# Splits of the last operands on GpSimd at a later place, source order of three engines at the first tiles, and another order of the last scalings

## The chip, the cores and the metric

One NeuronCore of a Trainium2 chip runs the whole program. Its engines work side by side, each from a queue of its own: TensorE (PE in the profile; its weight loads are PEld), VectorE (DVE), ScalarE (ACT), GpSimd (POOL), and SyncE (SP), which here only issues DMA transfers. The metric is the device time of one execution in microseconds, the median over runs.

## The reference

One layer of a hybrid decoder on 1024 tokens of width 1024, in float32:

```
u = rmsnorm(x, g0);  z = u @ w_in              # 1024 x 6048
o_attn = dilated attention of 3 head groups    # windows 128, 512, 2048; strides 1, 4, 16
o_rwkv = RWKV-7 time mixing of z               # 8 heads of 64, delta-rule state
merged = sigmoid(gate_a) * (o_attn @ w_attn_up) + sigmoid(gate_r) * (o_rwkv @ w_rwkv_up)
h = x + rmsnorm(merged @ w_out, g1)
h = h + rmsnorm(square(relu(rmsnorm(h, g2) @ w_ff_in)) @ w_ff_out, g3)
e = (p @ w_ple) * sigmoid(h @ w_ple_gate)
out = h + rmsnorm(e, g4)
```

The inputs are x, a per-layer embedding p (1024 x 256), the weights and the gains g0 to g4.

## The kernel before

**Split products.** A float32 product is made of three fast ones. Each operand is split into a high part (a copy, rounded to the format fp32r on the way) and a low part (the operand less its high part). `mm3` then issues high x high, high x low and low x high (L292, L294, L296 in the profile). A weight tile comes by `wload`: a DMA to `wr`, the copy to `wh` on ScalarE, the subtraction to `wl` on GpSimd. Since TensorE does three passes over everything, it is busy nearly all of the time, and the work of the others is laid beside it.

**Stages, in order.** First tiles: the eight 128-token tiles of x are loaded, normed, transposed and split to `uT`, while the first two column tiles of z are multiplied in quarters as tiles come ready. Then z column by column, with RWKV's small products between its matmuls, then attention's. Then the merges (the two up-projections times their gates, 8 of them), w_out in two halves of columns (`out_0`, `out_1` with the chain `mixed` behind each tile), the MLP (16 blocks, whose second product is done with seven instead of eight multiplications), its last block, and the gated embedding with the last norm, tile by tile (`finish`, `gate_mm`, `e_mm`).

**What sets the order.** TensorE's instructions always stand in source order. In most of the kernel that source order is made by a planner (`Order`): it keeps a clock and an end time for each engine, runs "dense" work (the large products) as filler, and puts the small products of the chains (generators that yield times) between as it thinks that their inputs are ready. The other four engines stand in source order only where a `manual_schedule` is open: from the start of the planner to the start of attention (`in_turn`), and from the first tile of the last MLP block to the end (`last["turn"]`). Everywhere else the framework's scheduler orders them by its own simulation, by readiness and then by source order; the first tiles are one such place, attention, the merges and the MLP another.

**First tiles** (in `layer`, ahead of the planner). For a tile i, `stats(i)` squares it on ScalarE with the sum of the row, takes the root there (which reads eps from the constants `cs`) and the reciprocal on VectorE. `u_tile(i)` scales it on VectorE (two inputs in SBUF: the tile and g0), transposes it in two halves of four on TensorE (`tp`), and splits each half to `uh` (copy on ScalarE) and `ul` (subtraction on VectorE). `z_quarter(n, q)` multiplies two tiles by column tile n. `keep_warm` gives TensorE products of ones at the start. In source order stand: stats of tiles 0 and 1, the first weights, tiles 0 and 1, stats of tile 2, the second weights, then for q of 0 to 3: z(0, q), the next two tiles, each behind the stats of the tile after it, z(1, q).

**Parked operands** (`park`, L968). The operands of the last products (w_ple, p, the last two rows of blocks of w_ff_out, w_ple_gate) are split early and kept in DRAM (`pk`), from where the end loads both parts. There are 14 pieces of 128 x 1024. Each is loaded to `MP`, copied on ScalarE and subtracted on VectorE into a tile of tag `BK2`, and stored. The chain starts when attention has turned the values of its second unit (`("vk", 1)`), and its pieces run among attention's work. A tag is one room of SBUF that tiles use in turn, in the order of the source; `ex` and `py` are two rooms of 512 columns that attention holds (its mask and its row statistics), and that the MLP takes for its sums later. `BK2` goes next to the third MLP weight (`third`) and then to w_ff_out.

**The end** (`e_mm`, L1749). For tile 7, the last, the product with the embedding is done in three column groups. VectorE multiplies it by the gate (`sg`), ScalarE squares it with the sum (`sc`), and `eg` is the product scaled by the gain g4: the first group on GpSimd, the others on VectorE. Then VectorE adds the three sums, ScalarE takes the root, VectorE the reciprocal and the three last fused multiply-adds, and each group is stored.

Of the kernel before, what the change touches and what calls it, by code (L numbers as in the profile page):

```python
# [10 lines left out]
F32 = mybir.dt.float32  # L11
F32R = mybir.dt.float32r
AF = mybir.ActivationFunctionType
OP = mybir.AluOpType
# [4 lines left out]
D = 1024  # L19
# [225 lines left out]
def layer(ctx: ExitStack, tc: tile.TileContext, x, pT, wz, wup, w_out, wff1, w_ff2, w_ple, w_pleg,  # L245
# [3 lines left out]
    sch = Order()  # L249
# [22 lines left out]
    done = set()  # L272
# [31 lines left out]
    def wait(cond):  # L304
        while not cond():
            yield 0.1
# [47 lines left out]
    with tc.tile_pool(name="xin", bufs=1) as xp:  # L354
        xts = [xp.tile([128, D], F32, name=f"xt{i}") for i in range(8)]

        def load_x(*tiles):
            for i in tiles:
                SY.dma_start(xts[i], x[i * 128:(i + 1) * 128, :])

        g1 = xp.tile([1, D], F32, name="g1")
        SY.dma_start(g1, gains[0:1, :])
        load_x(0, 1)
# [23 lines left out]
        def stats(i):  # L387
            ss = small.tile([128, 1], F32, name="ss")
            us = xp.tile([128, D], F32, name="us", bufs=4)
            S.activation(us, xts[i], AF.Square, accum_out=ss)  # L390
            ub[i] = us, rstd_of(ss, "rs")

        def u_tile(i):
            h, ts = i // 4, slice((i % 4) * 128, (i % 4) * 128 + 128)
            us, r = ub[i]
            V.scalar_tensor_tensor(us, xts[i], r, g0, op0=OP.mult, op1=OP.mult)
            for b in range(2):
                ps = psum.tile([128, 4, 128], F32, name="tp", tag=("m0", "m1", "s1", "s2")[tp[0] % 4])
                tp[0] += 1
                for k in range(4):  # L400
                    tr(ps[:, k, :], us[:, (4 * b + k) * 128:(4 * b + k + 1) * 128], 0.11)
                o = (slice(None), slice(4 * b, 4 * b + 4), ts)
                S.activation(uT[0][h][o], ps, AF.Copy)
                V.tensor_tensor(uT[1][h][o], ps, uT[0][h][o], OP.subtract)

        def z_quarter(n, q):
            h, ts = q // 2, slice((q % 2) * 256, (q % 2) * 256 + 256)
            if q % 2 == 0:
                zl[h].append(psum.tile([128, 512], F32, name="z", tag="s3") if h and n else zbank())
            hi, lo = wl[n]  # L410
            now(mm3(zl[h][n][:, ts], [(hi[:, k * 128:k * 128 + 128], lo[:, k * 128:k * 128 + 128],
                                       uT[0][h][:, k, ts], uT[1][h][:, k, ts]) for k in range(KT)]))

        stats(0)
        stats(1)
        wl = [wload(wz[0])]
        load_x(2)
        u_tile(0)
        u_tile(1)
        keep_warm(2)  # L420
        stats(2)
        wl.append(wload(wz[1]))
        load_x(3, 4, 5, 6, 7)
        pr = const.tile([128, N_PRM], F32, name="pr")
        SY.dma_start(pr, prm)
        omu = const.tile([128, 14], F32, name="omu")
        V.tensor_scalar(omu, pr[:, 0:14], -1.0, 1.0, op0=OP.mult, op1=OP.add)
        oka = const.tile([128, NU], F32, name="oka")
        V.tensor_scalar(oka, pr[:, P_KA:P_KA + NU], -1.0, 1.0, op0=OP.mult, op1=OP.add)
        for q in range(4):  # L430
            z_quarter(0, q)
            for i in (2 * q + 2, 2 * q + 3):
                if i < 7:
                    stats(i + 1)
                if i < 8:
                    u_tile(i)
            z_quarter(1, q)
# [529 lines left out]

    def park():  # L968

        yield from wait(lambda: ("vk", 1) in done)  # L970
        rows = lambda w, k: w[k * 128:(k + 1) * 128, :]
        half = lambda h: pT[:, halves[h]].rearrange("(k p) c -> p k c", p=128)
        for dst, src in ([(pk[1][:, k], rows(w_ple, k)) for k in range(2)]
                         + [(pk[1][:, 2 + h], half(h)) for h in range(2)]
                         + [(pk[2][:, k], rows(w_ff2, FF // 128 - 2 + k)) for k in range(2)]
                         + [(pk[0][:, k], rows(w_pleg, k)) for k in range(KT)]):
            raw = rtile([128, 1024], "pkr", "MP")
            land = SY.dma_start(raw if len(src.shape) == 2 else k2(raw), src)
            yield max(land - sch.t, 0.0)
            t = rtile([128, 2, 1024], "pk", "BK2", F32R)  # L980
            S.activation(t[:, 0], raw, AF.Copy)
            yield 1.0
            V.tensor_tensor(t[:, 1], raw, t[:, 0], OP.subtract)
            yield sch.until(V.end)
            yield max(SY.dma_start(dst, t.bitcast(F32)) - sch.t, 0.0)
            yield 3.0
        done.add("park")

    def attention():
# [759 lines left out]
    def e_mm(i):  # L1749
        def body():  # L1750
# [3 lines left out]
            for n, c in enumerate(cols):  # L1754
# [150 lines left out]
```

## Time and profile before

| | |
|---|---|
| median of 3 runs | 1781.07 us (1780.95 to 1781.54) |
| the profiled execution's own time | 1784.63 us |
| its span, first to last instruction | 1782.8 us |
| TensorE busy | 1751.7 us (98% of the span) |
| VectorE, ScalarE, GpSimd busy | 1069.6, 733.1, 735.0 us |
| parked pieces | first copy at 480.6, last at 663.9 us |
| merges | 840 to 905 us |
| last matmul starts | 1775.02 us |

The profile is of one execution. Its page gives busy times, a chain of work that ended last, and groups of instructions by line; the trace behind it can be asked for every instruction in order of time (start, duration, what it wrote and read, and in brackets how long its engine had been idle and who ended that), for the waits of an engine, and for the busy times of all engines in a stretch. Nearly every instruction of VectorE, ScalarE and GpSimd has line 113, a helper, so they are told apart by the names of their tiles, as `ul<-tp,uh`. A short name hides its number: `wh` is any of the high parts of weights. TensorE's gaps are where time can be won directly; a gap of another engine matters only where TensorE waits behind it.

### The profile page before, as it was taken

How to read it: one execution, taken by the hardware profiler on the slowest of the kernel's cores; microseconds unless marked ns; L12 is line 12 of the kernel's file. 1: busy time of each engine (PE TensorE's matmuls, PEld its weight loads, DVE VectorE, ACT ScalarE, POOL GpSimd, SP SyncE). 2: the span in 40 equal slices, each digit the busy share in tenths (PEclk: the TensorE clock that was granted, in tenths of full speed). 3: DMA queues.
4: the chain of work that ended last, by engine and by line, in shares of the span. 5: the costliest groups of instructions: out<-in, count | busy, mean ns of one | idle time of the engine just before them, and what ended most of it. 6: DMA issues, size and time to landing. Idle time of an engine off the chain costs nothing. (4 is left out here: it accounts for less than half of the span.)

```text
span 1782.8 us, 25896 instructions
## 1 busy us (share of the span) xinstructions
PE 1751.7 (98%) x10192; PEld 1431.0 (80%) x10192; DVE 1069.6 (60%) x1880; ACT 733.1 (41%) x1301; POOL 735.0 (41%) x485
## 2 busy tenths in 40 slices
PE   9999989999999999999999999999999999999998
PEld 8787877878877777777888888888888888888786
DVE  6289776757546343342744655565565677888643
ACT  5833333332345444452533533333333333333353
POOL 1354131221222323322230276666666797893211
PEclk9999999999999999999999999999999999999999
DMA  4621121212375543232632321111211121114611
GB/s 162 210 95 36 49 77 43 90 42 91 111 246 191 183 166 95 84 133 104 208 132 97 110 80 51 48 55 41 76 55 48 48 72 48 48 36 165 219 48 47
DMA packets 59322, 175.49 MB, mean 98 GB/s; under 512 B 6849, under 2 KB 7233, under 8 KB 56898
## 3 DMA queue, kind: packets, MB, share of 16 engines
q1 hardware_dynamic: 59202, 173.85, 29.0%
q8 instruction: 80, 1.31, 0.3%
q14 instruction: 40, 0.33, 0.1%
HBM read 125.20 MB, written 41.94 MB: 94 GB/s over the span
## 5 line engine op out<-in xcount | busy, mean ns | idle before, releaser
L113 DVE TENSOR_TENSOR tot<-tot,bk 128x512 f32<-128x512 f32 x468 | 308.1, 684 | 190.6 <-PE bk L296 189.8
L113 POOL TENSOR_TENSOR wl<-wr,wh 128x1024 fp32r<-128x1024 f32 (+1 forms) x87 | 211.5, 2431 | 436.2 <-ACT wh L113 412.2
L292 PE MATMUL z<-uh,wh 128*128 128x512 f32 (+1 forms) x800 | 314.9, 394 | 5.2 <-ACT part L113 3.0
L296 PE MATMUL z<-uh,wl 128*128 128x512 f32 (+1 forms) x800 | 314.5, 393 | 2.7 <-POOL wl L113 2.7
L294 PE MATMUL z<-ul,wh 128*128 128x512 f32 (+1 forms) x800 | 315.7, 395 | 0.0
L294 PE MATMUL z<-f,wh 128*128 128x512 f32 x496 | 193.1, 389 | 0.2 <-DVE f L113 0.2
L292 PE MATMUL z<-f,wh 128*128 128x512 f32 x496 | 193.2, 389 | 0.1
L296 PE MATMUL z<-f,wl 128*128 128x512 f32 x496 | 193.0, 389 | 0.0
L113 ACT ACTIVATE duo<-sum 128x512 fp32r<-128x512 f32 x150 | 90.5, 626 | 224.9 <-PE bk L296 113.3
L292 PEld LDWEIGHTS z<-uh,wh 128*128 128x128 f32 x800 | 152.6, 191 | 36.9 <-ACT part L113 3.5
L296 PEld LDWEIGHTS z<-uh,wl 128*128 128x128 f32 x800 | 152.6, 191 | 34.5 <-POOL wl L113 4.0
L294 PEld LDWEIGHTS z<-ul,wh 128*128 128x128 f32 x800 | 152.8, 191 | 30.7 <-issue 3.8
L292 PE MATMUL bk<-duo 128*128 128x512 f32 x420 | 163.4, 389 | 0.0
L294 PE MATMUL bk<-duo 128*128 128x512 f32 x420 | 163.4, 389 | 0.0
L296 PE MATMUL bk<-duo 128*128 128x512 f32 x420 | 163.4, 389 | 0.0
L113 POOL TENSOR_TENSOR duo<-sum,duo 128x512 fp32r<-128x512 f32 x75 | 100.7, 1343 | 95.6 <-ACT duo L113 95.6
L113 ACT ACTIVATE wh<-wr 128x1024 fp32r<-128x1024 f32 (+1 forms) x87 | 90.3, 1038 | 103.7 <-PE z L294 74.6
L113 POOL TENSOR_TENSOR sum<-w2r 128x512 f32<-128x512 f32 x75 | 99.1, 1321 | 65.1 <-DMA w2r<-in_w_ff_dram 60.3
L294 PEld LDWEIGHTS z<-f,wh 128*128 128x128 f32 x496 | 93.1, 188 | 19.8 <-DVE f L113 0.5
L292 PEld LDWEIGHTS z<-f,wh 128*128 128x128 f32 x496 | 93.1, 188 | 19.6 <-ACT f L113 0.3
L296 PEld LDWEIGHTS z<-f,wl 128*128 128x128 f32 x496 | 93.1, 188 | 19.3
L113 POOL TENSOR_TENSOR sum<-hr 128x512 f32<-128x512 f32 x75 | 97.6, 1310 | 4.8 <-DVE duo L113 3.1
(310 smaller groups left out, 3198.1 us busy)
## 6 DMA issues: line engine op xcount, KB each, us to landing
wr<-in_wz_dram SPq DMA_DIRECT2D x48, 512.0 KB, 4.0
wr<-in_wff_dram SPq DMA_DIRECT2D x31, 512.0 KB, 3.6
w2r<-in_w_ff_dram SPq DMA_DIRECT2D x30, 512.0 KB, 3.7
xt<-in_x_dram SPq DMA_DIRECT2D x16, 512.0 KB, 4.2
gscr<-gst SPq DMA_DIRECT2D x32, 256.0 KB, 2.1
pkg<-pk SPq DMA_DIRECT2D x8, 1024.0 KB, 4.5
g<-gscr SPq DMA_DIRECT2D x16, 512.0 KB, 4.2
wpg<-pkg SPq DMA_DIRECT2D x16, 512.0 KB, 6.6
```

What stands on the lines that cost most here:

```text
L113: return f(*a, **kw)
L292: PE.matmul(ps, ah, bh, start=i == 0, stop=False)
L294: PE.matmul(ps, ah, bl, start=False, stop=False)
L296: PE.matmul(ps, al, bh, start=False, stop=i == n - 1)
```

## The change

It has three parts.

1. At the first tiles a `manual_schedule` is opened for VectorE, ScalarE and GpSimd (not SyncE), so that they, too, run in source order until the last z quarter. The scaling moves out of `u_tile` into `scale(i)`, called right behind `stats(i)`. The second weights are asked for before tiles 0 and 1 are transposed, and the scaling of tile 2 stands behind those. The load of `pr` and the two small products from it (`omu`, `oka`) stand behind the z quarters.
2. `park` starts when attention has combined its first half (`("A", 0)`). Its pieces are loaded in two halves of columns into the rooms `ex` and `py`; GpSimd makes both the copy and the subtraction of each half, in four instructions a piece. ScalarE and VectorE have no part in it. A piece is stored as before, and the pause behind a store is 1.0 instead of the transfer and 3.0.
3. For tile 7 in `e_mm` the scaling of the second column group stands between the two additions, and that of the third behind the root.

```
+        first_turn = tc.manual_schedule(engines=OTHERS - {mybir.EngineType.SP})
+        first_turn.__enter__()
...
+        def scale(i):
+            us, r = ub[i]
+            V.scalar_tensor_tensor(us, xts[i], r, g0, op0=OP.mult, op1=OP.mult)
...
-        stats(0)
-        stats(1)
+        for i in range(2):
+            stats(i)
+            scale(i)
         wl = [wload(wz[0])]
         load_x(2)
-        u_tile(0)
-        u_tile(1)
-        keep_warm(2)
         stats(2)
         wl.append(wload(wz[1]))
         load_x(3, 4, 5, 6, 7)
+        u_tile(0)
+        u_tile(1)
+        scale(2)
+        keep_warm(2)
+        for q in range(4):
+            z_quarter(0, q)
+            for i in (2 * q + 2, 2 * q + 3):
+                if i < 7:
+                    stats(i + 1)
+                    scale(i + 1)
+                if i < 8:
+                    u_tile(i)
+            z_quarter(1, q)
+        first_turn.__exit__(None, None, None)
         pr = const.tile([128, N_PRM], F32, name="pr")
...
-        yield from wait(lambda: ("vk", 1) in done)
+        yield from wait(lambda: ("A", 0) in done)
...
-            raw = rtile([128, 1024], "pkr", "MP")
-            land = SY.dma_start(raw if len(src.shape) == 2 else k2(raw), src)
+            raw = [rtile([128, 512], "pkr", x) for x in ("ex", "py")]
+            for c in range(2):
+                land = SY.dma_start(raw[c], src[:, halves[c]] if len(src.shape) == 2 else src[:, c])
             yield max(land - sch.t, 0.0)
             t = rtile([128, 2, 1024], "pk", "BK2", F32R)
-            S.activation(t[:, 0], raw, AF.Copy)
+            for c in range(2):
+                hi = t[:, 0, halves[c]]
+                G.tensor_copy(hi, raw[c])
+                G.tensor_tensor(t[:, 1, halves[c]], raw[c], hi, OP.subtract)
+            yield sch.until(G.end)
+            SY.dma_start(dst, t.bitcast(F32))
             yield 1.0
-            V.tensor_tensor(t[:, 1], raw, t[:, 0], OP.subtract)
-            yield sch.until(V.end)
-            yield max(SY.dma_start(dst, t.bitcast(F32)) - sch.t, 0.0)
-            yield 3.0
...
-            for c in cols[1:] if i == 7 else ():
-                V.tensor_tensor(eg[:, c], sg[:, c], P["g4"][:, c], OP.mult)
+            scale = lambda c: V.tensor_tensor(eg[:, c], sg[:, c], P["g4"][:, c], OP.mult)
             for n in range(1, len(cols)):
+                if i == 7 and n == 2:
+                    scale(cols[1])
                 V.tensor_tensor(sc[:, n:n + 1], sc[:, n - 1:n], sc[:, n:n + 1], OP.add)
-            r = rstd_of(sc[:, n:n + 1], "rs")
+            if i == 7:
+                r = small.tile([128, 1], F32, name="rs")
+                S.activation(r, sc[:, n:n + 1], AF.Sqrt, bias=eps, scale=1.0 / D)
+                scale(cols[2])
+                V.reciprocal(r, r)
+            else:
+                r = rstd_of(sc[:, n:n + 1], "rs")
```

More of the change, by code (lines that the diff above doesn't have):

```diff
@@ L391, in stats @@
             ub[i] = us, rstd_of(ss, "rs")
+        def scale(i):
+            us, r = ub[i]
+            V.scalar_tensor_tensor(us, xts[i], r, g0, op0=OP.mult, op1=OP.mult)
         def u_tile(i):
             h, ts = i // 4, slice((i % 4) * 128, (i % 4) * 128 + 128)
-            us, r = ub[i]
-            V.scalar_tensor_tensor(us, xts[i], r, g0, op0=OP.mult, op1=OP.mult)
+            us = ub[i][0]
             for b in range(2):
@@ L429, in layer @@
         V.tensor_scalar(oka, pr[:, P_KA:P_KA + NU], -1.0, 1.0, op0=OP.mult, op1=OP.add)
[L430 to L437, printed above, removed]
     rt = ctx.enter_context(tc.tile_pool(name="rt", bufs=1, reuse_waits="tile"))
```

## The prediction

> **What bounds the kernel now.** I read the page first, then the TensorE waits, then the three places that the change touches.
>
> ```profile
> span 1782.8 us, 25896 instructions
> ...
> PE 1751.7 (98%) x10192; PEld 1431.0 (80%) x10192; DVE 1069.6 (60%) x1880; ACT 733.1 (41%) x1301; POOL 735.0 (41%) x485
> ```
>
> TensorE (PE) is busy for 1751.7 of 1782.8 us, so an edit that leaves its work alone can take away 31 us at most: its gaps and the tail after its last matmul. The list of TensorE waits names who ends them:
>
> ```profile
> PE yt L283 <- ACT rb L113: 2.0, 1, 2.0
> PE pt L283 <- ACT SB L113: 1.5, 2, 1.0
> ...
> PE sc L275 <- DVE qk L113: 1.1, 1, 1.1
> ```
>
> Columns: total us, times, longest. These three lie in attention. A table by stage shows what attention loses and what the merges, the stage that inherits the parked splits, lose:
>
> ```profile
> 505.00:670.00 165.00, 158.21 (x896) 122.67 (x897) 75.08 (x190) 80.67 (x171) 43.83 (x17) 1.00 0.56 191
> ...
> 840.00:905.00 65.00, 65.00 (x289) 53.80 (x288) 45.68 (x63) 32.39 (x40) 14.99 (x8) 1.00 0.55 190
> ```
>
> After the stretch and its length stand PE, PEld, DVE, ACT and POOL busy. Attention leaves PE idle 165.00 - 158.21 = 6.8 us; the merges leave it no gap at all, with DVE at 45.68 of 65 us and POOL at 14.99.
>
> **First tiles: source order on DVE, ACT and POOL.** The timeline of the first 25 us, engine after engine (start, us, what, idle before):
>
> ```profile
> 9.92 1.92 PE L283 MATMUL tp<-cs,us 128*128 128x128 f32 x8
> 12.66 1.97 PE L283 MATMUL tp<-cs,us 128*128 128x128 f32 x8 [0.82 <-DVE us L113]
> ...
> 18.57 1.03 PE L283 MATMUL tp<-cs,us 128*128 128x128 f32 x8
> 20.86 1.06 PE L283 MATMUL tp<-cs,us 128*128 128x128 f32 x8 [1.26 <-DVE rs L113]
> 21.68 0.36 PE L292 MATMUL z<-uh,wh 128*128 128x256 f32 x1
> ```
> ```profile
> 7.49 0.28 DVE L113 SCALAR_TENSOR_TENSOR cen<-cs 128x128 f32<-128x128 f32 x1
> ...
> 9.27 3.33 DVE L113 SCALAR_TENSOR_TENSOR us<-xt,rs,g 128x1024 f32<-128x1024 f32 x1
> ...
> 16.09 1.28 DVE L113 SCALAR_TENSOR_TENSOR us<-xt,rs,g 128x1024 f32<-128x1024 f32 x1
> ...
> 17.99 2.73 DVE L113 SCALAR_TENSOR_TENSOR us<-xt,rs,g 128x1024 f32<-128x1024 f32 x1
> ...
> 22.02 2.48 DVE L113 TENSOR_TENSOR ul<-tp,uh 128x512 fp32r<-128x512 f32 x4
> ```
> ```profile
> 9.17 2.36 POOL L113 TENSOR_TENSOR wl<-wr,wh 128x1024 fp32r<-128x1024 f32 x1 [8.71 <-ACT wh L113]
> 16.47 3.17 POOL L113 TENSOR_TENSOR wl<-wr,wh 128x1024 fp32r<-128x1024 f32 x1 [4.94 <-ACT wh L113]
> ```
> ```profile
> 6.97 0.46 ACT L113 ACTIVATE rs<-ss,cs 128x1 f32<-128x1 f32 x2
> 8.03 1.06 ACT L113 ACTIVATE wh<-wr 128x1024 fp32r<-128x1024 f32 x1 [0.60 <-DMA wr<-in_wz_dram]
> ...
> 17.66 1.04 ACT L113 ACTIVATE us<-xt 128x1024 f32<-128x1024 f32 x1
> ...
> 18.83 0.29 ACT L113 ACTIVATE rs<-ss,cs 128x1 f32<-128x1 f32 x1
> 19.20 1.08 ACT L113 ACTIVATE uh<-tp 128x512 fp32r<-128x512 f32 x2
> ```
>
> A scaling (two SBUF inputs) takes 1.28 us when it starts ahead of a POOL subtraction (16.09) and 3.33 or 2.73 when it starts behind one (9.27 behind 9.17, 17.99 behind 16.47): whichever engine gets in first holds the other off until it is done. The stalled scalings are what tiles 1 and 3 wait for, 0.82 and 1.26 us of PE.
>
> In source order the second scaling follows the first at 9.27, up to 0.2 us sooner without cen (0.28) in front. On ACT the square of tile 1 now stands behind the root of tile 0. The pair of roots stands at 6.97; I place the first at 6.6, then square 1.06, accumulator and root make wh start some 0.1 us later than 8.03 and wl at about 9.3. So the scaling gets in first and ends near 10.4. Tile 1's transposes then follow tile 0's at 11.84 rather than 12.66, and the first z quarter starts 0.8 us sooner. It is still at half speed there (eight transposes take 1.92, later 1.03), so at tile 2 about 0.6 us remain: 17.95. The third scaling and wl of the second weights no longer meet: that subtraction follows the first at 12.7 and ends at 15.1. The fourth scaling ends near 17.8, so tile 3 follows tile 2 at once and z(1,0) starts at 19.9, against 21.7 before.
>
> Then source order takes something back. The queue of ACT now reads: copies of tile 2, square and root of tile 4, copies of tile 3; that of DVE: subtractions of tile 2, scaling of tile 4, subtractions of tile 3. From the start of tile 2's transposes: copies end at +1.7 (0.63 after 18.57, then 1.08), square and root to +3.1 (18.83 + 0.29 less 17.66 is 1.46), scaling to +4.6 (1.28), first subtraction to +5.2 (2.48/4). PE wants it at 1.03 + 0.82 (20.86 to 21.68) + 24 x 0.12 + 0.12 = +4.85. It waits 0.3 to 0.4 us, and again at tiles 4 and 5; tiles 6 and 7 have no square between. The moves of pr, omu and oka cost nothing: 0.3 us of DVE and one load, used only after the z quarters; if that cover fails, their 0.3 us.
>
> Sum: 17.95 + 5.3 = 23.25, where before stood 21.68 + 24 x 0.12 + 0.12 = 24.68: -1.4, then +0.35 for the second such wait: **-1.1**. What could add to it is the clock:
>
> ```profile
> 15.92 0.41 PE L292 MATMUL z<-uh,wh 128*128 128x256 f32 x1
> ...
> 16.29 0.28 PE L296 MATMUL z<-uh,wl 128*128 128x256 f32 x1
> 16.41 0.28 PE L292 MATMUL z<-uh,wh 128*128 128x256 f32 x1
> ```
>
> PE turns to full speed between these rows (at full speed such a matmul starts every 0.12 us, 16.29 to 16.41, the step used above), some 3.5 us after the gap at 12.66 ended. Without that gap it can turn as much sooner; tile 2 then starts near 17.05 and the sum is -2.0. I take **-1.5**; the bounds are -0.4 (POOL gets the port first, tile 1 as before) and -2.0. The Trainium skill, TensorE: Matmul & The Clock Gate, Part 1, has the clock released after one busy window of about 3.4 us that runs free of the kernel; by that rule the sum is -2.0 in about half of the executions, which no single trace here can show.
>
> **The parked operands.** Fourteen pieces leave ACT and DVE in attention. What they cost PE there:
>
> ```profile
> 509.68 1.06 ACT L113 ACTIVATE pk<-pkr 128x1024 fp32r<-128x1024 f32 x1 [4.64 <-DMA pkr<-in_pT_dram]
> ...
> 539.75 1.04 ACT L113 ACTIVATE pk<-pkr 128x1024 fp32r<-128x1024 f32 x1
> ```
> ```profile
> 510.77 1.23 DVE L113 TENSOR_TENSOR pk<-pkr,pk 128x1024 fp32r<-128x1024 f32 x1 [7.23 <-ACT pk L113]
> 511.91 0.20 DVE L113 RECIPROCAL vc<-vc 128x8 f32<-128x8 f32 x1
> ...
> 609.92 3.41 DVE L113 TENSOR_TENSOR pk<-pkr,pk 128x1024 fp32r<-128x1024 f32 x1
> ```
>
> The reciprocal on which rb hangs stands behind a parked subtraction (yt, 2.0 us); a parked copy sits between the exponentials for the first pt (1.0); a subtraction of 3.41 us sits ahead of the rotation for sc (1.1). With the other pt wait, 0.5, that is **-4.6** of the 6.8. TensorE's order is written by the planner, which no longer counts this work, so the stream is shuffled; I let 0.7 of new waits come in (bounds 0 and 2.2, what stays of the 6.8).
>
> The new place starts as attention's tiles ex and py come free and runs through the merges. One piece is four POOL instructions. Half a subtraction costs 2.36/2, about 1.2 to 1.3 us; the copy isn't in the trace: between half of that (one input instead of two) and all of it; I take 1.0. So a piece holds POOL for 2 x (1.0 + 1.25) = 4.5 us (3.7 to 5.0), and POOL is taken about half of the time, as each piece also waits for its loads and for the store ahead of it (4.5 us, below). Fourteen of some 10 us are done about 140 to 160 us later, near 950, before the next user of BK2.
>
> ```profile
> pkg<-pk SPq DMA_DIRECT2D x8, 1024.0 KB, 4.5
> ```
>
> What stands behind it: the lo part of each merge's weights, on the same queue.
>
> ```profile
> 862.23 1.84 POOL L113 TENSOR_TENSOR wl<-wr,wh 128x768 fp32r<-128x768 f32 x1 [11.13 <-ACT wh L113]
> ```
> ```profile
> 865.07 0.39 PE L296 MATMUL bk<-orw,wl 128*128 128x512 f32 x1
> ```
>
> This one ends at 864.07 and is read at 865.07: 1.0 us of slack. Behind half-taken POOL it is late by 0 to 4.5 us, 1.1 on average, and the four DVE subtractions of wo ahead of it, which now meet POOL's, bring it later still. I price the merges at **+1.9**: some 1.3 us here and 0.6 at the seven others. Bounds: 0, and 8 x (4.5 - 1.0) = 28 if every split stood behind a whole piece with no more slack than this one; I stay near the lower end, as PE waits nowhere in the merges now and POOL is half free. SP carries 28 loads for 14, also ahead of merge loads; in the same price. Net -4.6 + 0.7 + 1.9 = **-2.0**. The Trainium skill, GPSIMD Engine Reference, section 4.1, speaks against the move: elementwise work with two inputs belongs on VectorE, GpSimd being about twice as slow; the rows agree, 2.36 against 1.23 us. [...]
>
> **The last scalings.**
>
> ```profile
> 1775.74 0.95 DVE L113 TENSOR_TENSOR eg<-sg,g 128x256 f32<-128x256 f32 x2
> 1776.62 0.41 DVE L113 TENSOR_TENSOR sc<-sc 128x1 f32<-128x1 f32 x2
> ```
> ```profile
> 1776.18 0.19 ACT L113 ACTIVATION_READ_ACCUMULATOR bk<-sg 128x1 f32 x1
> 1777.06 0.29 ACT L113 ACTIVATE rs<-sc,cs 128x1 f32<-128x1 f32 x1 [0.70 <-DVE sc L113]
> ```
>
> Both scalings stand ahead of both additions; the root starts at 1777.06 though the last square's sum is there at 1776.37. In the new order the second addition can start near 1776.43 and the root at 1776.6; the moved scaling (0.4) lies beside the root (0.29 and the step to the reciprocal). **-0.45**, all of it on the chain that ends the kernel; bounds -0.2 and -0.6.
>
> **Sum.** -1.5 - 2.0 - 0.45 = -3.95, on a span of 1782.8, so 1778.85. The profiled execution itself took 1784.63 us and the median of the runs is 1781.07, 1.73 below the span; the median becomes **1777.1 us**.
>
> **Rivals.** (1) Nothing is lost at the merges and the clock opens sooner: -2.0 - 4.6 + 0.7 - 0.45, 1774.7. For it: POOL is at 14.99 of 65 us there; against: the 1.0 us slack. (2) The merges give back the gain of attention, +4.9 instead of +1.9: 1780.1. For it: DVE at 70% with two-input work that POOL will hold off. (3) The other side: on POOL's queue the lo split of every merge stands behind a whole piece. The rest of the change is worth -1.5 - 4.6 + 0.7 - 0.45 = -5.85, so at 0.75 us of wait for each of 8 merges the kernel is no faster, and from 1.2 each it is slower by more than 0.2%; at 1.4 the merges cost 11.2 instead of 1.9, 1786.4. Against it: most splits are ready well ahead, POOL half free. (4) The source order doesn't do what it says: POOL gets the port first at tile 1, -0.4 instead of -1.5, 1778.2. For it: 0.03 to 0.2 us decide.
>
> **How the numbers follow.** Forecast 0.45 (its own range 1775.3 to 1779.0), rivals 0.17, 0.19, 0.06, 0.13. A measurement here can tell 0.2%, 3.6 us: faster is below 1777.5, slower above 1784.6. Faster holds rival 1, a good half of the forecast and a little of 4 and 2: 0.50; slower is rival 3: 0.06; the rest 0.44. The range leaves out rival 3 and the ends of 1 and 2: 1773.0 to 1781.8.
>
> **What would show it.** Right: tile 1's scaling at 1.28 us and no gap ahead of the transposes of tiles 1 and 3; a wait of z for ul near 23 and 31 us; no parked work in attention, yt without its 2.0; POOL busy from 800 to 950 and small waits of bk or z for wl at the merges; the last root 0.45 us after where its squares end sooner. Wrong: waits for wl over 5 us in sum, new waits in attention over 2 us, or parked pieces still running past 1000, where DVE's chains feed the MLP.

## The result, and the profile after

The changed kernel takes **1792.52 us** (median of 5 runs, 1785.64 to 1795.28) against 1781.07 us (1780.95 to 1785.2): a ratio of **1.0053**, 95% interval 1.0029 to 1.0077. It is slower by 0.5%. The forecast was 1777.1 us, faster than before, with a range of 1773.0 to 1781.8. The profiled execution took 1793.29 us.

The page of the kernel after, its span:

```profile
span 1791.5 us, 25936 instructions
```

The table by stage of the kernel after, the same stretches and columns as in the prediction:

```profile
505.00:670.00 165.00, 162.93 (x914) 126.72 (x914) 61.60 (x201) 72.97 (x175) 44.58 (x17) 1.00 0.26 78
840.00:905.00 65.00, 53.84 (x209) 42.88 (x210) 38.81 (x48) 25.37 (x32) 27.30 (x20) 0.89 0.73 251
```

Attention now leaves TensorE idle 165.00 - 162.93 = 2.1 us, where it was 6.8. The merges, which left it no gap, now leave 11.2 us, at a mean granted clock of 0.89 instead of 1.00. What is left of attention's waits, from the list of TensorE waits between 505 and 780 us:

```profile
PE z L292 <- ACT qk L113: 1.2, 1, 1.2
PE pt L283 <- ACT SB L113: 0.6, 1, 0.6
```

yt and sc are gone, of pt 0.6 is left. The first tiles, timelines of TensorE, VectorE and GpSimd:

```profile
9.93 3.40 PE L283 MATMUL tp<-cs,us 128*128 128x128 f32 x16
...
14.50 0.39 PE L294 MATMUL z<-ul,wh 128*128 128x256 f32 x1 [0.56 <-DVE ul L113]
...
22.61 0.39 PE L294 MATMUL z<-ul,wh 128*128 128x256 f32 x1 [0.37 <-DVE ul L113]
...
30.73 0.39 PE L294 MATMUL z<-ul,wh 128*128 128x256 f32 x1 [0.37 <-DVE ul L113]
```
```profile
9.28 1.28 DVE L113 SCALAR_TENSOR_TENSOR us<-xt,rs,g 128x1024 f32<-128x1024 f32 x1
```
```profile
9.49 5.63 POOL L113 TENSOR_TENSOR wl<-wr,wh 128x1024 fp32r<-128x1024 f32 x2 [9.04 <-ACT wh L113]
```

The second scaling starts 0.2 us ahead of GpSimd's subtraction and takes 1.28 us instead of 3.33; the sixteen transposes of tiles 0 and 1 now run without a gap.

The whole loss lies in the merges. One row for each kernel shows it: the stretch from the first merge matmul (bk<-orw,wh) to the first matmul on wo (z<-wo,mt), by the timeline. First before, then after; the columns are start and end, length, then TensorE busy with its matmuls, weight loads, VectorE, ScalarE, GpSimd, the granted clock, the share of the DMA engines and GB/s.

```profile
840.14:905.44 65.30, 65.30 (x290) 54.06 (x289) 46.09 (x64) 32.39 (x40) 15.43 (x8) 1.00 0.56 192
```
```profile
830.77:914.80 84.03, 72.33 (x290) 57.54 (x288) 50.17 (x62) 31.01 (x40) 37.16 (x30) 0.92 0.73 250
```

The same 290 matmuls: 84.03 - 65.30 = **18.7 us** more, of which 84.03 - 72.33 = 11.7 is waiting and 72.33 - 65.30 = 7.0 is longer busy time of TensorE, most of it because matmuls ran slower. The kernel after starts the merges 9.4 us sooner (830.77 against 840.14) and ends them 9.4 us later. The four waits of TensorE there:

```profile
842.87 0.79 PE L296 MATMUL bk<-orw,wl 128*128 128x512 f32 x1 [3.33 <-POOL wl L113]
855.57 0.47 PE L292 MATMUL bk<-orw,wh 128*128 128x512 f32 x1 [3.30 <-DVE g L113]
869.53 0.66 PE L292 MATMUL bk<-orw,wh 128*128 128x512 f32 x1 [3.96 <-ACT wh L113]
871.64 0.80 PE L296 MATMUL bk<-orw,wl 128*128 128x512 f32 x1 [1.03 <-POOL wl L113]
```

The first three waits each close the clock. The table by stage for stretches behind them (the granted clock is the third number from the end):

```profile
842.90:845.70 2.80, 2.80 (x7) 2.22 (x8) 0.00 (x0) 0.00 (x0) 0.99 (x2) 0.50 0.95 317
...
856.20:859.40 3.20, 3.20 (x9) 2.52 (x8) 1.96 (x3) 1.06 (x1) 0.00 (x0) 0.50 0.81 182
869.80:876.40 6.60, 5.57 (x13) 3.88 (x13) 3.01 (x5) 3.89 (x5) 3.12 (x2) 0.50 0.89 314
```

It is granted at half for 3.4, 3.4 and 6.8 us, by the clock's record. TensorE works in some 12 of these 13.6 us (the first stretch begins at 842.41, inside the wait, and the last holds the wait of 1.03), so the clock costs some 6 of the 7.0 us above. What makes the rest isn't shown.

How the first wait arises is to be read on timelines of ScalarE, GpSimd and SyncE after, and of GpSimd and SyncE before:

```profile
830.79 0.85 ACT L113 ACTIVATE wh<-wr 128x768 fp32r<-128x768 f32 x1 [4.61 <-PE z L294]
```
```profile
836.41 0.61 POOL L113 CAST pk<-pkr 128x512 fp32r<-128x512 f32 x1 [4.07 <-DMA pkl<-pk]
...
839.03 1.59 POOL L113 TENSOR_TENSOR pk<-pkr,pk 128x512 fp32r<-128x512 f32 x1
840.58 2.25 POOL L113 TENSOR_TENSOR wl<-wr,wh 128x768 fp32r<-128x768 f32 x1
```
```profile
832.36 0.33 SPq L132 DMA_DIRECT2D pkl<-pk  x1
...
838.41 0.33 SPq L132 DMA_DIRECT2D pkr<-in_w_pleg_dram  x1
840.64 0.33 SPq L132 DMA_DIRECT2D pkl<-pk  x1
...
842.85 0.38 SPq L132 DMA_DIRECT2D wr<-in_w_out_dram  x1
```
```profile
841.09 1.84 POOL L113 TENSOR_TENSOR wl<-wr,wh 128x768 fp32r<-128x768 f32 x1 [9.04 <-ACT wh L113]
```
```profile
842.95 8.54 SPq L132 DMA_DIRECT2D wr<-in_w_out_dram  x3
```

wh is done at 831.64. Before, wl followed its wh at once (841.09, 0.95 us after the first merge matmul), but here a whole parked piece stands ahead of it on GpSimd's queue. That piece waits 4.07 us, with GpSimd idle, for the store that empties its room, and wl starts at 840.58, nine microseconds late. It frees the room wr only at 842.83, and SyncE issues the first load of w_out at 842.85. That is 12.1 us after the first merge matmul; before it was 842.95 - 840.14 = 2.8 us. There are two rooms wr, so each load waits for the split that frees its room. SyncE's waits between 830 and 915 us (total, times, longest) are led by it:

```profile
SPq L132 <- POOL wl L113: 21.9, 5, 8.3
```

So a late split makes the next loads late as well. And the loads land later, since the parked bytes share the DMA engines with them (their share of the stretch rose from 0.56 to 0.73). Median us from issue to landing between 830 and 915 us, before and after:

```profile
wr<-in_w_out_dram SPq DMA_DIRECT2D x8, 512.0 KB, 3.6
wr<-in_wup_dram SPq DMA_DIRECT2D x6, 384.0 KB, 3.1
```
```profile
wr<-in_w_out_dram SPq DMA_DIRECT2D x6, 512.0 KB, 4.7
wr<-in_wup_dram SPq DMA_DIRECT2D x5, 384.0 KB, 4.2
```

The last scalings, timeline of ScalarE after:

```profile
1785.76 0.19 ACT L113 ACTIVATION_READ_ACCUMULATOR bk<-sg 128x1 f32 x1
1786.17 0.29 ACT L113 ACTIVATE rs<-sc,cs 128x1 f32<-128x1 f32 x1 [0.23 <-DVE sc L113]
```

The root starts 0.41 us after the last square's sum begins to be read; before it was 1777.06 - 1776.18 = 0.88. Runs with the old order (e1, e3 below) have 0.89, e2 with the new one 0.41.

### The profile page after: what moved, and what is told of

Read it like the earlier page. It is cut to its first block, busy times and chain, and to the rows that moved or that the text cites. A ratio compares the mean times of both kernels' runs of the same rounds, so it can differ in the third digit from the quotient of the medians.

```text
span 1791.5 us, 25936 instructions
## 1 busy us (share of the span) xinstructions
PE 1755.4 (98%) x10192; PEld 1432.8 (80%) x10192; DVE 1050.8 (59%) x1866; ACT 717.7 (40%) x1287; POOL 793.8 (44%) x541
```

## The experiments

Seventeen kernels. The table takes the merges from the same row as above. Idle is length less TensorE busy; "first load" is the time from the first merge matmul to the issue of the first load of w_out, by SyncE's timeline. Ratios are to the kernel before on the same chip at the same time (its medians there were 1781.7 to 1782.9).

| kernel | median us | ratio, 95% interval | merges us | idle us | first load us |
|---|---|---|---|---|---|
| before | 1781.07 | | 65.3 | 0 | 2.8 |
| after | 1792.52 | 1.0053 (1.0029 to 1.0077) | 84.0 | 11.7 | 12.1 |
| e1 first tiles alone | 1782.35 | 0.9996 (0.9982 to 1.0011) | 66.3 | 0.4 | 2.8 |
| e2 first tiles and last scalings | 1781.31 | 0.9989 (0.9978 to 0.9999) | 66.9 | 1.0 | 2.8 |
| e3 parking alone | 1796.60 | 1.0082 (1.0068 to 1.0096) | 84.7 | 12.9 | 13.0 |
| e4 parked splits on ScalarE, VectorE | 1792.70 | 1.0061 (1.0048 to 1.0074) | 73.2 | 6.5 | 2.8 |
| e5 parked transfers, no splits | 1783.24 | 1.0002 (0.9985 to 1.0019) | 73.4 | 5.1 | 3.1 |
| e6 parked splits, no transfers | 1803.35 | 1.0117 (1.0095 to 1.0140) | 89.2 | 15.9 | 16.6 |
| e7 two rooms a half | 1794.45 | 1.0069 (1.0047 to 1.0091) | 79.0 | 9.6 | 9.6 |
| e8 pause after seven pieces | 1812.69 | 1.0173 (1.0147 to 1.0198) | 84.4 | 10.6 | 12.0 |
| e11 parked transfers on GpSimd's queue | 1824.23 | 1.0237 (1.0218 to 1.0257) | 105.4 | 26.8 | 14.9 |
| e12 merges' lo splits on VectorE | 1790.76 | 1.0050 (1.0035 to 1.0065) | 83.0 | 11.6 | 11.2 |
| e13 the same without late parking | 1780.61 | 0.9990 (0.9974 to 1.0005) | 65.3 | 0 | 1.9 |
| e14 both queues cleared | 1797.04 | 1.0078 (1.0064 to 1.0093) | 76.9 | 8.3 | 3.0 |
| e15 the same without late parking | 1781.53 | 0.9993 (0.9982 to 1.0005) | 65.3 | 0 | 1.8 |

e9, e10, e16 and e17 leave the parked work in attention and are told at the end of the section.

**Parts alone.** e1 takes the first hunks of the diff (source order), e2 adds the last hunk (scalings), e3 takes park() alone.

> Only the source order at the first tiles; parking and the last scalings as before. Theory (the loss lies in the merges alone): this part is a gain of its own, as the trace of the changed kernel stands 1.3 to 1.4 us ahead from 54 to 228 us; time 1778.5 to 1780 us, TensorE's waits of 1.3 and 0.8 us for the scalings gone, three waits of 0.3 to 0.6 for ul in their place. Rival (the moved start disturbs the stages that follow, for instance through the clock's windows): 1781 us or more, with other throttled stretches than those of before at 153, 231, 265 and 364 us.

> The whole change without the parking: first tiles and last scalings. Theory: 0.4 to 0.5 us below the run with the first tiles alone, so 1778 to 1779.5 us, and its runs lie within 1 us of each other, as those of the kernel before mostly do. Rival (the last scalings cost something, or gain nothing, since the store behind them waits anyway): the same time as with the first tiles alone.

> Only the parking moved to GpSimd and behind attention. Theory: the whole loss, so 1788 to 1797 us, runs several us apart, TensorE over 9 us idle between 830 and 915 us with two to four throttled stretches there, and attention 6 us or more sooner than before. Rival (the loss needs the shift by the first tiles, as the two phases of clock and loads must meet): under 1784 us.

Parking alone is slower by 0.8%, and its merges take 84.7 us: the whole loss, without the shift by the first tiles. The other two parts together gain 0.1%, which is hardly told from nothing. e1 and e2 both miss their expected times, and e2's eleven runs lie 7.5 us apart (1777.13 to 1784.62), not within 1 us. e3 also shows something of the first tiles, though it leaves them as before. Its transposes, timeline of TensorE, and the first split of weights, timeline of ScalarE:

```profile
9.93 2.67 PE L283 MATMUL tp<-cs,us 128*128 128x128 f32 x16
```
```profile
8.33 1.06 ACT L113 ACTIVATE wh<-wr 128x1024 fp32r<-128x1024 f32 x1 [0.91 <-DMA wr<-in_wz_dram]
```

Sixteen take 2.67 us in one row here, where before the first eight took 1.92 and the next eight, after a gap, 1.97. In e3 the first weights landed later, so wh started at 8.33 instead of 8.03 and GpSimd's subtraction at 9.47 instead of 9.17. The second scaling (9.28) now stood ahead of it, took 1.28 us instead of 3.33, and the gap at tile 1 was gone, without the new order. The clock opened at 11.5 us, not at 16.2. The first matmul on lo (the work after the z quarters) comes at 54.64 us in e3, against 55.40 before and 54.01 after. So of the 1.4 us that the two profiles show for the first tiles, 0.8 is the bad luck of the one execution that was profiled before, in which the first weights came 0.3 us sooner, and 0.6 is left for the order. Over the seventeen profiles with the new order this matmul comes at 53.84 to 54.41 us.

**Which engine splits.** e4 keeps the new place, rooms, loads and stores, but

```
-                G.tensor_copy(hi, raw[c])
-                G.tensor_tensor(t[:, 1, halves[c]], raw[c], hi, OP.subtract)
...
+                S.activation(hi, raw[c], AF.Copy)
+                V.tensor_tensor(t[:, 1, halves[c]], raw[c], hi, OP.subtract)
```

> The whole change, but the parked pieces are copied on ScalarE and subtracted on VectorE as before, in the new place and the new rooms, with the same loads and stores. Theory (GpSimd's queue, in order, holds the merges' lo parts behind parked copies that wait for their loads): GpSimd has no parked work, so no wait for wl or wh over 1 us at the merges, TensorE under 3 us idle from 830 to 915 us, time 1770 to 1776 us. Rival 1 (the loads and stores, on SyncE's queue and the rings, do the harm): the loss stays, 1785 us or more. Rival 2 (VectorE, 70% busy there, can't carry more): waits for g and mt of over 5 us, 1780 us or more.

```profile
829.20:902.39 73.19, 66.68 (x290) 53.67 (x288) 49.42 (x67) 34.43 (x45) 13.26 (x7) 1.00 0.75 253
```

The expected 1770 to 1776 us fails. GpSimd is back at 13.26 us and the first load at 2.8 us, and the merges still take 7.9 us more than before. The time is no better than after, because ScalarE's and VectorE's parked work is late further on: from the first matmul on wo to the first on f 99.5 us instead of 91.6 (one wait of 4.91 us at 912.22 for ACT mt), and from there to the first on duo another 4.2. GpSimd's queue alone is therefore not the cause of the total.

**Transfers without splits, splits without transfers.** e5 stores each raw half straight back into the places of its hi and lo part; the parked split is left out of the computation.

```
-                G.tensor_copy(hi, raw[c])
-                G.tensor_tensor(t[:, 1, halves[c]], raw[c], hi, OP.subtract)
...
-            SY.dma_start(dst, t.bitcast(F32))
...
+                SY.dma_start(dst[:, :, halves[c]], raw[c][:, None, :].to_broadcast([128, 2, 512]))
```

> Whole change, but the parked pieces are not split: each raw half is stored straight back, into the place of its hi and of its lo part (28 stores of 512 KB for 14 of 1 MB; the parked split is left out of the computation). GpSimd has no parked work, SyncE and the rings keep all of it. Theory A (on GpSimd's in-order queue the lo splits of the merges stand behind parked instructions that wait for a load or a store): the wait of the merges for wl goes, the merges are back to 65 to 68 us between the first merge matmul and the first z of wo (before 65.3, whole change 84.0), and the time is 1770 to 1777. Theory B (the parked loads and stores themselves make the merges' own loads late, whichever engine splits): the merges stay at 73 us or more, with waits for g and wh, and the time is 1780 to 1790. Both in part: 68 to 73 us.

```profile
832.16:905.58 73.42, 68.35 (x290) 55.61 (x289) 47.89 (x62) 31.88 (x40) 15.81 (x8) 0.95 0.77 275
```

e6 is the opposite: the pieces are split from a source that is loaded once, with a 128x2x8 corner stored; the parked buffers get the raw operand in both parts by plain copies, and the parked split is left out of what the kernel computes. Two things stand otherwise than the expectation says: there were 20 pieces, and the copies, free of any wait, ran at 15 to 98 us.

> GpSimd does the parked copies and subtractions, 18 pieces at the new place, but from one source that is loaded once, and stores a 128 x 2 x 8 corner of each; the parked buffers are filled by plain copies between buffers in attention at the old place (both parts hold the raw operand: the parked split is left out of the computation). GpSimd has the work without waits for loads at the head of its queue. Theory A in its narrow form (waiting at the head of the queue, not the work): merges 65 to 69 us, time 1770 to 1777. If the work itself holds wl up (busy GpSimd): merges 72 us or more with waits for wl, time 1780 or more. Theory B (transfers): merges 65 to 68 us.

```profile
833.08:922.29 89.21, 73.34 (x289) 57.63 (x288) 56.08 (x63) 33.31 (x41) 68.88 (x55) 0.92 0.47 149
```
```profile
845.38 2.48 POOL L113 TENSOR_TENSOR pk<-pkr,pk 128x512 fp32r<-128x512 f32 x2
847.82 1.80 POOL L113 TENSOR_TENSOR wl<-wr,wh 128x768 fp32r<-128x768 f32 x1
```

Either half does harm by itself. The transfers alone cost 8.1 us in the merges with the share of the DMA engines at 0.77, though the whole of e5 takes no longer than the kernel before, as it starts the merges 8.0 us sooner (832.16 against 840.14). The splits alone cost 23.9 us with that share at 0.47, below the 0.56 of before, and with GpSimd busy for 68.88 of 89.21 us, wl mostly behind two halves of a piece. That is denser than after, with 37.16 of 84.03, so 23.9 isn't the share that the splits have there. The narrow theory (only waiting for DMA at the head of the queue hurts, not the work) falls with e6 for work that dense; how much the work alone costs at the density of after isn't shown.

**Spacing it.** e7 takes two raw rooms for each half and stores half a piece at a time; e8 holds the room of the parked pieces after the seventh until the last merge is done.

```
+            if n == 7:
+                hold = rtile([128, 16], "hold", "BK2")
+                yield from wait(lambda: "merged" in done)
+                V.tensor_copy(hold[:, 0:1], mT[1][1][:, 7, 511:512].bitcast(F32))
```

> Whole change with two raw rooms for each half (the tiles ex, py and yc, pg in turn) and a store of 512 KB for each half, so that the next piece is loaded while one is split. Theory A: the parked instructions rarely wait at the head of GpSimd's queue; the merges take 65 to 72 us and the time is 1773 to 1781. Theory B: the same bytes in less time, denser at the first merges; the merges take 76 us or more, and the time is 1784 to 1795.

> Whole change, but after seven pieces the room of the parked operands is held until the last merge is done; the other seven pieces follow then. Both theories: the merges are back to 65 to 68 us; the loss of 18.7 us there goes. Open is what the seven later pieces cost: if nothing, 1770 to 1777, faster than before; if the loss only moves on to the MLP's first chains (waits of f and duo for DVE or for weights), 1780 to 1790.

```profile
828.40:912.84 84.44, 73.87 (x290) 58.70 (x289) 48.19 (x61) 30.91 (x40) 23.55 (x18) 0.90 0.58 204
```
```profile
848.32 2.29 POOL L113 TENSOR_TENSOR wl<-wr,wh 128x768 fp32r<-128x768 f32 x1
866.80 1.82 POOL L113 TENSOR_TENSOR wl<-wr,wh 128x768 fp32r<-128x768 f32 x1 [16.19 <-ACT wh L113]
```

e7 comes out as theory B has it, 79.0 us and 1794.45. e8 missed what both theories expected, and tells most. No parked split runs between 848.4 and 923.2 us, so the parked splits take only the first 20 us of the merges, and these still take 84.4 us, as after. The first wl is late (a wait of 3.25 us at 840.43), the first load goes out at 12.0 us, and from 848.4 GpSimd itself waits for weights. A late start is carried through the rest; the harm isn't in proportion to the parked work that runs beside the merges. The seven later pieces cost another 20 us, 111.7 instead of 91.6 from wo to f: they ran until 979 us, and TensorE waited 16.90 us at 988.09 for DVE hh.

**Clearing the queues.** e11 lets GpSimd issue the parked loads and stores, e12 lets VectorE make the merges' eight lo splits, e14 does both and takes GpSimd's other work between 770 and 950 us to VectorE as well; e13 and e15 are controls with parking as before.

```
+    SG = Loads(nc.gpsimd, sch)
...
-                land = SY.dma_start(raw[c], src[:, halves[c]] if len(src.shape) == 2 else src[:, c])
+                land = SG.dma_start(raw[c], src[:, halves[c]] if len(src.shape) == 2 else src[:, c])
...
-            SY.dma_start(dst, t.bitcast(F32))
+            SG.dma_start(dst, t.bitcast(F32))
```

and, in e12 and e13 (e14 and e15 in the same way, by a count of the loads),

```
-            G.tensor_tensor(lo[:, :n], raw[:, :n], hi[:, :n], OP.subtract)
+            (V if n == 768 else G).tensor_tensor(lo[:, :n], raw[:, :n], hi[:, :n], OP.subtract)
```

> Whole change, but GpSimd issues the parked loads and stores itself, behind its own splits; SyncE's queue holds none of them. GpSimd's work and its waits for landing stay, the bytes stay. If the parked transfers hurt by standing ahead of the merges' loads on SyncE's in-order queue (waits for pk there: 18.6 us between 830 and 915), the merges fall from 84.0 to 76 us or less and the time to 1778 to 1786. If they hurt by sharing the rings, or if GpSimd's queue does all of the harm, the merges stay at 80 us or more and the time at 1789 or more.

> Whole change, but the lo splits of the merges' weights (eight subtractions of 128x768) are made by VectorE and so leave GpSimd's queue; the parked work, its rooms and its transfers are as changed. If those splits, standing behind parked work on GpSimd's in-order queue, are what makes the merges late, the merges fall from 84.0 us to about the 73 us that the two runs without parked work on GpSimd showed, waits for wl are gone, and the time is 1779 to 1785. If GpSimd's work hurts by holding VectorE off (or the transfers do it all), the merges stay at 80 us or more and the time at 1789 or more.

> Control for the run before: first tiles and last scalings as changed, parking as in the kernel before, and the lo splits of the merges' weights on VectorE. It gives what the move of these splits costs by itself. VectorE is busy 45.7 of 65 us in the merges and gets some 7 us more: merges 65 to 69 us, time 1778 to 1784.

> Whole change, with the parked loads and stores issued by GpSimd and everything else that GpSimd has between 770 and 950 us given to VectorE (three splits of 128x1024 and four other operations before the merges, the eight lo splits of the merges, four of wo). So neither SyncE's nor GpSimd's queue holds parked work ahead of anything that the merges read; the bytes, the parked splits and their times on GpSimd stay. If the order of the two queues is the whole cause (each alone only moves the wait to the other), the merges are back to 65 to 69 us and the time is 1772 to 1779, better than both kernels. If the rings or GpSimd's hold on VectorE cost as much as the queues, the merges stay at 72 us or more, and the time at 1781 or more.

> Control: first tiles and last scalings as changed, parking as in the kernel before, and the same operations given from GpSimd to VectorE. Merges 65 to 69 us, time 1777 to 1783; what it loses against the run with the first tiles and the last scalings alone (1781.3) is the price of the move to VectorE.

e11, SyncE's waits between 770 and 950 us (total, times, longest):

```profile
SPq L132 <- POOL wl L113: 86.7, 9, 14.4
```

With all of it on one queue, wl is later still, and SyncE, rid of the parked transfers, waits for wl instead. e12, the row of the merges, then ScalarE's and SyncE's timelines:

```profile
828.14:911.14 83.00, 71.41 (x290) 57.53 (x288) 54.47 (x68) 31.12 (x39) 26.88 (x24) 0.92 0.75 264
```
```profile
845.37 1.06 ACT L113 ACTIVATE wo<-wr 128x1024 fp32r<-128x1024 f32 x1 [15.88 <-DMA wr<-in_w_out_dram]
```
```profile
836.05 0.33 SPq L132 DMA_DIRECT2D pkr<-in_w_pleg_dram  x1
838.45 0.33 SPq L132 DMA_DIRECT2D pkl<-pk  x1
...
839.34 0.87 SPq L132 DMA_DIRECT2D wr<-in_w_out_dram  x1
```

Here no wl stands on GpSimd's queue, and the first load of w_out is as late as after (11.2 us): it stands on SyncE's queue behind a parked load and a parked store, which wait for GpSimd's splits. ScalarE idles 15.88 us for it. Each queue alone is enough to make this load late. e14 clears both:

```profile
832.60:909.45 76.85, 68.56 (x289) 55.32 (x288) 49.06 (x65) 28.69 (x37) 41.88 (x52) 0.96 0.85 302
```
```profile
wr<-in_w_out_dram SPq DMA_DIRECT2D x7, 512.0 KB, 6.4
wr<-in_wup_dram SPq DMA_DIRECT2D x5, 384.0 KB, 5.2
```

The first load is back at 3.0 us, and the merges fall from 84.0 to 76.9. They are 11.6 us above their control, though, with landing times of 6.4 and 5.2 us instead of 3.6 and 3.1. The expectation of 65 to 69 us fails: the order of the queues is not the whole cause. What stays are the shared DMA engines and GpSimd's hold on VectorE, which e14 doesn't take apart; and it packs more into the stretch than after (a share of 0.85 and 302 GB/s against 0.73 and 250). (Further on e14 loses 9 us more against its control, 102.7 against 93.2 us from wo to f.) On the landing the Trainium skill, DMA: Bandwidth & Descriptors, "Issuing engines are not separate DMA queues", says that transfers started by different engines run on the same sixteen DMA engines and interleave; the trace of e14 agrees, 6.4 us with the parked transfers on a queue of their own.

**The gain without the loss.** e9 and e10 leave the parked work in attention but give both halves of the split (e9) or only the subtraction (e10) to GpSimd; e16 and e17 leave it on ScalarE and VectorE with a later gate. All have the new first tiles and last scalings.

> First tiles and last scalings as changed; the parked splits stay at the old place (in attention, one raw room of 128x1024, loads and stores as before), but GpSimd makes both the copy and the subtraction there instead of ScalarE and VectorE. If attention's waits came from the engines that split (copy ahead of the exponentials, subtraction ahead of the reciprocal), they go without the merges paying: attention gains some 4.6 us, the merges stay at 65 to 67 us, and the time is 1774 to 1779, better than both kernels. If attention has no cover for 14 x 3.6 = 50 us more of GpSimd (43.8 of 165 us busy there) new waits for GpSimd appear in attention and the time is 1781 or more.

> As the run before, but ScalarE keeps the copy and GpSimd takes only the subtraction. The waits for yt (2.0 us, reciprocal behind a subtraction) and sc (1.1) should go, the waits for pt (1.0 and 0.5, copy between exponentials) stay: attention gains about 3 us, merges as before, 1775 to 1780. If GpSimd's subtraction of 128x1024 holds VectorE off for 2.4 us at a bad place, 1781 or more.

> First tiles and last scalings as changed; the parked splits stay in attention on ScalarE and VectorE, in their old rooms, but begin one block of attention later (gate on the third block instead of the second), well ahead of the merges. If attention's waits hang on which instructions the parked splits happen to stand ahead of, the block that had most of them is free, the merges stay at 65 to 67 us, and the time is 1775 to 1779. If they only come in later blocks, 1779 to 1783.

> As the run before, two blocks later (gate on the fourth block). Same two readings: 1775 to 1779 if attention's waits go, 1779 to 1783 if they come later; and if the last pieces reach the merges, the merges are longer than 67 us and the time 1783 or more.

e9 took 1789.76 us (1.0042, 1.0027 to 1.0057), e10 1778.93 (0.9990, 0.9978 to 1.0002), e16 1788.14 (1.0026, 1.0015 to 1.0037), e17 1787.83 (1.0027, 1.0013 to 1.0042). The merges are short in all (65.9 to 66.7 us). In e9 GpSimd's product for the rotation (sw, at 612.22) now stands behind a parked piece, and VectorE's last step of it waits 4.60 us; the TensorE waits of e9 in attention:

```profile
PE sc L275 <- DVE qk L113: 7.1, 2, 5.7
```

In e16 and e17 the gate moved nothing: the pieces ran from 479 and 475 us, as before from 481, since they go as soon as their raw room is free. And yet both are slower by 0.3%, with e2's parking but for the gate. One of their waits hangs on what a parked instruction happens to stand ahead of. VectorE's timeline of e17:

```profile
505.43 1.23 DVE L113 TENSOR_TENSOR pk<-pkr,pk 128x1024 fp32r<-128x1024 f32 x1 [9.63 <-ACT pk L113]
506.57 0.20 DVE L113 RECIPROCAL vc<-vc 128x8 f32<-128x8 f32 x1
```

This is the collision that the prediction read (yt waits 2.1 us in e17, and not in e2). Their longest wait is another: sc waits 6.1 us for DVE qk, and in e17 GpSimd's product behind it (sw, at 657.97) stands behind a split of weights that came at 655.66, with no parked piece between. How the gate led to that is open. None of these kernels beats the kernel before by more than a measurement can tell; e2, e10 and e13, with parking in attention, stand at 0.999.

## Why the prediction was wrong

**First tiles, -1.5.** Measured -1.4 between the two profiles, by the steps foreseen: the scaling got in first, the gap at tile 1 went, and z waits 0.37 us at 22.61 and 30.73 (0.3 to 0.4 foreseen; the steps give 5.2 where the sum takes 5.3). Not foreseen was the 0.56 at 14.50. Rival 4 didn't come: in all seventeen profiles with the new order the second scaling takes 1.28 or 1.29 us. But 0.8 of the 1.4 is the luck of the one execution profiled before, and e1 shows no difference (0.9996). A term of a microsecond was read from one draw of something that varies by as much; that the profiles agree with it is luck in part. The Trainium skill, TensorE: Matmul & The Clock Gate, Part 1, has the clock's window run free of the kernel, and the seventeen profiles agree: on the same first instructions the clock opens between 9.72 and 12.97 us. The -2.0 that the prediction drew from it for half of the executions came in none (53.84 us at best, -1.6 against the profile before): where the clock opens early, TensorE waits for ScalarE's copies instead, 1.36 us for uh at 13.55 in e1.

**Parking, attention's side, -4.6 + 0.7.** Idle time fell by 6.8 - 2.1 = 4.7 us, with yt and sc gone and no new wait: right in its mechanism, and the 0.7 wasn't needed. The same matmuls up to the end of attention took 6.1 us less, though (below), as TensorE's busy time fell by another 1.4, which the prediction didn't have.

**Parking, the merges' side, +1.9: the step that failed.** It measured **+18.7**. The prediction had the right place, GpSimd's queue ahead of wl, and the slack of 1.0 us. What it had wrong is the wait (how late wl comes) and the path (what hangs on it), and it put the parked transfers at nothing of their own.

(1) It weighed GpSimd's busy time ("POOL half free") and not the time at the head of its queue. A parked copy that waits 4.07 us for a store holds wl up as well as one that runs. Rival 3 had this mechanism, at 0.75 us a merge as the point where it decides, but it got a chance of 0.06 with the argument that GpSimd was half free.

(2) The pieces ran from 772.6 to 952.0 us and so through all of the merges, as the prediction had it, but it took these as eight separate splits, each late by 1.1 us on average. They are one chain through two rooms wr and SyncE's queue: the wait of wl sets when the next weights are loaded. e8 shows that lateness in the first 20 us is enough for the whole loss. Even the prediction's own sign of being wrong, waits for wl over 5 us in sum, misses it: TensorE waits 4.4 us for wl, and the other 7.3 us of waiting came further along the chain, for g and wh. In the table, where the first load goes out by 3.1 us the merges take 65 to 77 us; at 9.6 us 79; from 11.2 to 13.0 us 83 to 85; at 14.9 and 16.6 us 105 and 89.

(3) It priced "28 loads for 14" at nothing of its own. The parked transfers alone cost 8.1 us (e5), 7.9 in e4 and 11.6 in e14 against its control.

A part of each is the clock. In after, some 6 of the 18.7 us is half speed that follows waits of 3.3 to 4.0 us. The Trainium skill, TensorE: Matmul & The Clock Gate, "Why this matters for your kernels", warns of idle gaps over some 3 us between matmul bursts; the rows at 842.87, 855.57 and 869.53 agree, and the prediction, whose bound of 28 us counted waits alone, left it out.

Queue order and transfers can't be taken apart exactly: 84.0 falls to 76.9 when the queues are cleared (e14) and to 73.2 or 73.4 when GpSimd's splits are gone (e4, e5), so what goes with the queues is worth 7 to 11 us and what stays with the transfers 8 to 12, with the clock in both. Whether the later landings alone make the 8 us of e5, or also SyncE's waits for its own parked stores, stays open, and so does what GpSimd's hold on VectorE adds in after and in e14.

**Last scalings, -0.45.** Measured 0.41 - 0.88 = -0.47: right, and the same in e2 against e1 (0.41 and 0.89). A gain of this size can't be told in the medians.

**The sum.** -1.4 at the first tiles, -1.5 between 54 and 238 us (a half-speed stretch of 3.4 us at 231 us that the profile before has and the one after has not), -6.1 to the end of attention and -0.4 to the merges, +18.7 there, +0.2 to the last matmul and -0.9 behind it (-0.47 of it up to the root) make +8.6; the spans differ by 8.7.

## What to carry over

Before work is moved onto a queue with spare busy time, ask what each of its instructions waits for, and what would then stand behind it: an in-order queue is taken from the moment its head waits, so busy time isn't its load. Where a stage is a chain through few rooms, with a slack of 1 us at its tightest split, the price of a late start isn't its own wait alone, but the waits that it causes along the chain, and the clock that closes behind them; read the slack of the first link, and what the moved transfers add to the landing of the stage's own loads. And a gain read from one profiled execution should be asked whether a run of the same code could show it.

## What the runs showed of the hardware

- A wait of 3.30 us (855.57) was followed by 3.4 us at half clock, one of 3.96 us (869.53) by 6.8 us; shorter ones mostly were not, but in e2 a wait of 1.89 us near 1680 us closed the clock for 3.4 us where one of 2.14 us in e1 did not.
- The clock's first opening came between 9.7 and 16.2 us over these nineteen profiles. From there on every stretch of its record up to the last is a multiple of 3.41 us long, open or half. Half-speed stretches of 3.4 or 6.8 us near 152, 231 and 362 us are there in some of them and not in others, also where the code up to there is the same (e2 and e12). Each is worth up to 1.7 or 3.4 us, as much as the terms argued over here.
- GpSimd's copy of 128x512 took 0.61 us (the prediction took 1.0), its subtraction 1.29: a piece holds it for 3.8 us, not 4.5. The merges were late all the same.
